# Larger and alternating chunks in four buffers, with graded ends, in a streaming softmax with relative position bias

## The chip, the cores and the metric

The kernel runs on one core of one Trainium2 chip. The metric is the device time of one execution in microseconds (us). Times are medians of several executions, with the range. An execution counts as *fast* unless it lies more than 1.5% above the fastest of the same kernel, and ratios use fast runs alone. The granted TensorE clock was 1.00 of full speed (this kernel uses no TensorE). All outputs are right.

Hardware facts below come from the profiles and traces. Where the Trainium skill (the notes on the chip) is drawn on, it is named with its page.

## The reference

The kernel adds a bias that depends only on the distance between query and key, clipped to 16, and takes a softmax over each row. All is float32.

```python
B, H, S = (2, 8, 2112); max_rel = 16
pos = np.arange(S)
rel = np.clip(pos[:, None] - pos[None, :], -max_rel, max_rel) + max_rel
logits = logits + rel_bias[:, rel][None]      # (2, 8, 2112, 2112)
logits = logits - logits.max(axis=-1, keepdims=True)
exp = np.exp(logits)
out = exp / exp.sum(axis=-1, keepdims=True)
```

There are 2 x 8 x 2112 rows of 2112 numbers (8,448 bytes). 285 MB go in and 285 MB go out, and little is computed on each number, so this is a streaming kernel. (The kernel leaves out the maximum, which these inputs don't need.)

## The kernel before

Two heads share the 128 partitions. A partition holds 33 neighbouring rows of one head; they are worked on in *chunks* of 3 rows, so a load or a store moves 128 pieces of 3 x 8,448 = 25,344 bytes. There are seven chunk buffers (`bufs=7`), hence 21 rows in memory. A buffer goes through: load, add of the bias (VectorE), three exponentials with row sums (ScalarE), reciprocal and three scalings (VectorE), store. Then the buffer is free for the load of the chunk seven later.

```python
R = 3
io = ctx.enter_context(tc.tile_pool(name="io", bufs=7))
...
NPRE = 2
pre = [load(c, nc.sync) for c in chunks[:NPRE]]       # first loads: SyncE's queue
rbB = const.tile([P, H // 2, 2, W], FP32, tag="rbB")
nc.scalar.dma_start(out=rbB, in_=...)                 # bias table
...                                                   # cut: bias_rows(k), the bias row F
for n, c in enumerate(chunks):
    k, row, j, r = c
    if k != fk:
        F, fk = bias_rows(k), k                       # every 22 chunks
    L = pre[n] if n < NPRE else load(c, nc.gpsimd)    # other loads: GpSimd's queue
    ...                                               # cut: the views L3, F3
    nc.vector.tensor_tensor(out=L3, in0=L3, in1=F3, op=ALU.add)
    tot = small.tile([P, R], FP32, tag="tot", name="tot")
    for i in range(r):
        x = L[:, i * S : (i + 1) * S]
        nc.scalar.activation(out=x, in_=x, func=EXP, accum_out=tot[:, i : i + 1])
    nc.vector.reciprocal(out=tot[:, 0:r], in_=tot[:, 0:r])
    for i in range(r):
        x = L[:, i * S : (i + 1) * S]
        nc.vector.tensor_scalar_mul(out=x, in0=x, scalar1=tot[:, i : i + 1])
    nc.sync.dma_start(out=rows(out, row, j, r), in_=L[:, 0 : r * S])   # store
```

One thing isn't visible in this text. The framework's scheduler decides in which order the instructions stand on each engine; the program text gives dependences only. An engine works through its own list in order. On VectorE the list has, for nearly all chunks, the scaling of one chunk *behind* the adds of the next two chunks.

The softmax here doesn't subtract the row's maximum and nothing guards it: scores larger than these inputs give would overflow.

Of the kernel before, what the change touches and what calls it, by code (L numbers as in the profile page):

```python
# [1 line left out]

# [4 lines left out]

FP32 = mybir.dt.float32
EXP = mybir.ActivationFunctionType.Exp
ALU = mybir.AluOpType  # L10


@with_exitstack
def kernel(
    ctx: ExitStack,
    tc: tile.TileContext,
    logits: bass.AP,
    rel_bias: bass.AP,
    out: bass.AP,
):  # L20




    nc = tc.nc
    P = 128
    B, H, S, S2 = logits.shape
    assert S == S2
    MR = 16
    W = 2 * MR + 1  # L30
    NB = S // W
    assert NB * W == S and 2 * NB == P and H % 2 == 0
    R = 3
    FW = S + W - 1

    const = ctx.enter_context(tc.tile_pool(name="const", bufs=1))
    fpool = ctx.enter_context(tc.tile_pool(name="fpool", bufs=2))
    io = ctx.enter_context(tc.tile_pool(name="io", bufs=7))
    small = ctx.enter_context(tc.tile_pool(name="small", bufs=8))

    chunks = []
    for k in range(H // 2):
        for b in range(B):
            last = k == H // 2 - 1 and b == B - 1
            sizes = [R] * (W // R)
            if last:
                sizes = sizes[:-1] + [1] * R
            j = 0
            for r in sizes:
                chunks.append((k, (b * H + 2 * k) * S, j, r))  # L50
                j += r
            assert j == W

    def rows(t, row, j, r):
        return bass.AP(
            tensor=t.tensor,
            offset=t.offset + (row + j) * S,
            ap=[[W * S, P], [1, r * S]],
        )

    def load(c, eng):
        k, row, j, r = c
        L = io.tile([P, R * S], FP32, tag="L", name="L")
        eng.dma_start(out=L[:, 0 : r * S], in_=rows(logits, row, j, r))  # L64
        return L

    NPRE = 2
    pre = [load(c, nc.sync) for c in chunks[:NPRE]]

    rbB = const.tile([P, H // 2, 2, W], FP32, tag="rbB")  # L70
    nc.scalar.dma_start(
        out=rbB,
        in_=bass.AP(tensor=rel_bias.tensor, offset=rel_bias.offset, ap=[[0, P], [1, H * W]]),
    )

    qm = const.tile([P, NB], FP32, tag="qm")
    for p0 in (0, NB):
        nc.gpsimd.iota(  # L78
            qm[p0 : p0 + NB],
            pattern=[[-1, NB]],  # L80
            base=0,
            channel_multiplier=1,
            allow_small_or_imprecise_dtypes=True,
        )
    eq = const.tile([P, NB], FP32, tag="eq")
    lt = const.tile([P, NB], FP32, tag="lt")
    gt = const.tile([P, NB], FP32, tag="gt")
    for m, op in ((eq, ALU.is_equal), (lt, ALU.is_gt), (gt, ALU.is_lt)):
        nc.vector.tensor_scalar(out=m, in0=qm, scalar1=0.0, scalar2=None, op0=op)  # L89
    rbP = const.tile([P, H // 2, W], FP32, tag="rbP")  # L90
    nc.vector.tensor_copy(out=rbP[0:NB], in_=rbB[0:NB, :, 0, :])  # L91
    nc.vector.tensor_copy(out=rbP[NB:P], in_=rbB[NB:P, :, 1, :])  # L92

    def bias_rows(k):

        F = fpool.tile([P, FW], FP32, tag="F", name="F")
        low = rbP[:, k, W - 1 : W]
        high = rbP[:, k, 0:1]
        rest = small.tile([P, NB], FP32, tag="rest", name="rest", bufs=2)
        nc.vector.tensor_scalar(out=rest, in0=lt, scalar1=low, scalar2=None, op0=ALU.mult)  # L100
        nc.vector.scalar_tensor_tensor(  # L101
            out=rest, in0=gt, scalar=high, in1=rest, op0=ALU.mult, op1=ALU.add
        )
        pitch = list(F.ap[0])[0]
        blocks = bass.AP(
            tensor=F.tensor, offset=F.offset + MR, ap=[[pitch, P], [W, NB], [1, W]]
        )
        rpitch = list(rbP.ap[0])[0]
        rev = bass.AP(
            tensor=rbP.tensor,  # L110
            offset=rbP.offset + k * W + W - 1,
            ap=[[rpitch, P], [0, NB], [-1, W]],
        )

        def wide(t):
            return bass.AP(
                tensor=t.tensor, offset=t.offset, ap=[[list(t.ap[0])[0], P], [1, NB], [0, W]]
            )

        nc.vector.tensor_tensor(out=blocks, in0=wide(eq), in1=rev, op=ALU.mult)  # L120
        nc.vector.tensor_tensor(out=blocks, in0=blocks, in1=wide(rest), op=ALU.add)  # L121
        nc.vector.tensor_copy(out=F[:, 0:MR], in_=low.to_broadcast([P, MR]))  # L122
        nc.vector.tensor_copy(out=F[:, FW - MR : FW], in_=high.to_broadcast([P, MR]))  # L123
        return F

    F, fk = None, None
    for n, c in enumerate(chunks):
        k, row, j, r = c
        if k != fk:
            F, fk = bias_rows(k), k  # L130
        L = pre[n] if n < NPRE else load(c, nc.gpsimd)
        pitch = list(L.ap[0])[0]
        L3 = bass.AP(tensor=L.tensor, offset=L.offset, ap=[[pitch, P], [S, r], [1, S]])

        F3 = bass.AP(
            tensor=F.tensor,
            offset=F.offset + W - 1 - j,
            ap=[[list(F.ap[0])[0], P], [-1, r], [1, S]],
        )
        nc.vector.tensor_tensor(out=L3, in0=L3, in1=F3, op=ALU.add)  # L140
        tot = small.tile([P, R], FP32, tag="tot", name="tot")
        for i in range(r):
            x = L[:, i * S : (i + 1) * S]
            nc.scalar.activation(out=x, in_=x, func=EXP, accum_out=tot[:, i : i + 1])  # L144
        nc.vector.reciprocal(out=tot[:, 0:r], in_=tot[:, 0:r])  # L145
        for i in range(r):
            x = L[:, i * S : (i + 1) * S]
            nc.vector.tensor_scalar_mul(out=x, in0=x, scalar1=tot[:, i : i + 1])  # L148
        nc.sync.dma_start(out=rows(out, row, j, r), in_=L[:, 0 : r * S])


# [1 line left out]
_INS = ['logits', 'rel_bias']  # L153
_OUTS = [((2, 8, 2112, 2112), 'float32')]


# [23 lines left out]
```

## Time and profile before

| | before |
|---|---|
| time | 1334.06 us (1333.89 to 1334.34, 6 runs) |
| span of the profiled run | 1332.3 us |
| VectorE busy, ScalarE busy | 71%, 39% |
| bytes moved, mean rate | 571.19 MB, 429 GB/s |
| first store issued | 57.0 us |

These are lines of the profile page of the kernel before. The row "GB/s" has 40 equal slices of the span. Below "## 5" a group reads: line, engine, operation, shapes, count, then busy time and mean nanoseconds of one, then idle time ahead of it and what ended it. Below "## 6" are transfers: count, size, median time from issue to landing.

```profile
DVE 947.2 (71%) x473; ACT 524.9 (39%) x529; POOL 49.0 (4%) x94
...
DMA  9999999999999999999999999999999999999998
GB/s 392 415 402 432 432 435 431 434 431 434 431 434 430 434 431 433 432 432 434 432 434 430 434 432 433 432 434 431 433 434 432 432 432 434 431 432 432 433 428 372
...
DMA 79%; DVE 11%; issue 7%; another core or an unknown queue 1%; ACT 0%; POOLq 0%; POOL 0%; ACTq 0%
...
L140 DVE TENSOR_TENSOR L<-L,F 128x6336 f32<-128x6336 f32 (+1 forms) x90 | 594.7, 6609 | 346.8 <-DMA L<-in_logits_dram 346.6
L148 DVE TENSOR_SCALAR L<-L,tot 128x2112 f32<-128x2112 f32 x264 | 331.8, 1313 | 0.0
...
out_dram<-L SPq DMA_DIRECT2D x87, 3168.0 KB, 38.2
L<-in_logits_dram POOLq DMA_DIRECT2D x85, 3168.0 KB, 25.7
```

The DMA engines are the limit: their row is at nine tenths throughout, the rate is flat between 430 and 435 GB/s from the fourth slice to the 38th, and the chain of waits is 79% DMA. VectorE waits for loads (346.6 us ahead of the adds).

### The profile page before, as it was taken

What the parts mean: (1) busy time and instruction counts of PE and PEld (TensorE: products, weight loads), DVE (VectorE), ACT (ScalarE), POOL (GpSimd) and SP (SyncE); (2) the same over time, 40 slices, a digit from 0 to 9 for tenths busy, and PEclk for the clock granted to TensorE, in tenths of its full rate; (3) what the DMA queues carried; (4) which work ended last, traced back from release to release, by engine and by line L of the source; (5) the groups of instructions that cost most, each with busy time, mean ns of one, the idle gap of its engine ahead of it and who ended that gap; (6) DMA issues with size and microseconds to landing.
All of it is one profiled execution on the core that took longest, in us unless ns stands there. A gap on an engine that the chain in (4) does not pass through costs nothing.

```text
span 1332.3 us, 1666 instructions
## 1 busy us (share of the span) xinstructions
DVE 947.2 (71%) x473; ACT 524.9 (39%) x529; POOL 49.0 (4%) x94
## 2 busy tenths in 40 slices
DVE  4997677669676677767966677766796677766773
ACT  0754334433344333443344333443334333443341
POOL 0000000000000000000000000000000000000000
DMA  9999999999999999999999999999999999999998
GB/s 392 415 402 432 432 435 431 434 431 434 431 434 430 434 431 433 432 432 434 432 434 430 434 432 433 432 434 431 433 434 432 432 432 434 431 432 432 433 428 372
DMA packets 26076, 571.19 MB, mean 429 GB/s; under 512 B 2896, under 2 KB 3024, under 8 KB 3024
## 3 DMA queue, kind: packets, MB, share of 16 engines
q1 hardware_dynamic: 13248, 291.97, 51.0%
q0 software_dynamic: 12672, 278.99, 48.8%
q10 hardware_dynamic: 144, 0.14, 0.0%
q14 instruction: 12, 0.10, 0.0%
HBM read 285.61 MB, written 285.47 MB: 429 GB/s over the span
## 4 chain that ended last, share of the span: by engine, by line
DMA 79%; DVE 11%; issue 7%; another core or an unknown queue 1%; ACT 0%; POOLq 0%; POOL 0%; ACTq 0%
DMA out_dram<-L 47%; DMA L<-in_logits_dram 30%; DVE L L148 6%; DVE L L140 4%; DMA rbB<-in_rel_bias_dram 1%; DVE F L121 0%; DVE F L120 0%; ACT L L144 0%; DVE tot L145 0%; POOLq L64 0%; POOL L L64 0%; DVE rest L100 0%; DVE rest L101 0%; DVE rbP L92 0%
## 5 line engine op out<-in xcount | busy, mean ns | idle before, releaser
L140 DVE TENSOR_TENSOR L<-L,F 128x6336 f32<-128x6336 f32 (+1 forms) x90 | 594.7, 6609 | 346.8 <-DMA L<-in_logits_dram 346.6
L144 ACT ACTIVATE L<-L 128x2112 f32<-128x2112 f32 x264 | 515.2, 1952 | 768.7 <-DVE L L140 756.5
L148 DVE TENSOR_SCALAR L<-L,tot 128x2112 f32<-128x2112 f32 x264 | 331.8, 1313 | 0.0
L64 POOL DMA_DIRECT2D L<-in_logits_dram x88 | 48.5, 551 | 1241.2 <-DMA out_dram<-L 1231.6
L144 ACT ACTIVATION_READ_ACCUMULATOR L<-L 128x1 f32 x264 | 49.2, 186 | 0.0
L145 DVE RECIPROCAL tot<-tot 128x3 f32<-128x3 f32 (+1 forms) x90 | 14.8, 167 | 0.9 <-ACT L L144 0.9
L91 DVE COPY rbP<-rbB 64x132 f32<-64x132 f32 x1 | 0.2, 223 | 17.9 <-DMA rbB<-in_rel_bias_dram 17.9
L121 DVE TENSOR_TENSOR F<-F,rest 128x2112 f32<-128x2112 f32 x4 | 9.4, 2344 | 0.0
L120 DVE TENSOR_TENSOR F<-eq,rbP 128x2112 f32<-128x2112 f32 x4 | 9.4, 2344 | 0.0
L144 ACT ACT_TABLE_LOAD x1 | 1.3, 1283 | 17.8 <-DMA L<-in_logits_dram 17.8
L101 DVE SCALAR_TENSOR_TENSOR rest<-gt,rbP,rest 128x64 f32<-128x64 f32 x4 | 1.0, 265 | 0.0
L100 DVE TENSOR_SCALAR rest<-lt,rbP 128x64 f32<-128x64 f32 x4 | 0.9, 240 | 0.0
L122 DVE COPY F<-rbP 128x16 f32<-128x16 f32 x4 | 0.7, 163 | 0.0
L123 DVE COPY F<-rbP 128x16 f32<-128x16 f32 x4 | 0.7, 167 | 0.0
L78 POOL IOTA qm<- 64x64 f32 x2 | 0.4, 176 | 0.4 <-PEq L175 0.4
L92 DVE COPY rbP<-rbB 64x132 f32<-64x132 f32 x1 | 0.2, 225 | 0.0
L89 DVE TENSOR_SCALAR lt<-qm 128x64 f32<-128x64 f32 x1 | 0.2, 186 | 0.0
L89 DVE TENSOR_SCALAR gt<-qm 128x64 f32<-128x64 f32 x1 | 0.2, 186 | 0.0
L89 DVE TENSOR_SCALAR eq<-qm 128x64 f32<-128x64 f32 x1 | 0.2, 185 | 0.0
L164 POOL MEMSET const-float32-0.0<- 128x1 f32 x1 | 0.1, 98 | 0.2 <-issue 0.2
L164 POOL MEMSET const-bfloat16-1.0<- 128x1 bf16 x1 | 0.1, 101 | 0.0
L164 POOL MEMSET const-float32-1.0<- 128x1 f32 x1 | 0.1, 98 | 0.0
(1 smaller groups left out, 0.1 us busy)
## 6 DMA issues: line engine op xcount, KB each, us to landing
out_dram<-L SPq DMA_DIRECT2D x87, 3168.0 KB, 38.2
L<-in_logits_dram POOLq DMA_DIRECT2D x85, 3168.0 KB, 25.7
L<-in_logits_dram SPq DMA_DIRECT2D x2, 3168.0 KB, 24.3
L<-in_logits_dram POOLq DMA_DIRECT2D x3, 1056.0 KB, 17.0
out_dram<-L SPq DMA_DIRECT2D x3, 1056.0 KB, 18.3
rbB<-in_rel_bias_dram ACTq DMA_DIRECT2D x1, 132.0 KB, 17.2
```

The source lines that it names most:

```text
L64: eng.dma_start(out=L[:, 0 : r * S], in_=rows(logits, row, j, r))
L89: nc.vector.tensor_scalar(out=m, in0=qm, scalar1=0.0, scalar2=None, op0=op)
L100: nc.vector.tensor_scalar(out=rest, in0=lt, scalar1=low, scalar2=None, op0=ALU.mult)
L101: nc.vector.scalar_tensor_tensor(out=rest, in0=gt, scalar=high, in1=rest, op0=ALU.mult, op1=ALU.add)
L120: nc.vector.tensor_tensor(out=blocks, in0=wide(eq), in1=rev, op=ALU.mult)
L121: nc.vector.tensor_tensor(out=blocks, in0=blocks, in1=wide(rest), op=ALU.add)
L122: nc.vector.tensor_copy(out=F[:, 0:MR], in_=low.to_broadcast([P, MR]))
L123: nc.vector.tensor_copy(out=F[:, FW - MR : FW], in_=high.to_broadcast([P, MR]))
L140: nc.vector.tensor_tensor(out=L3, in0=L3, in1=F3, op=ALU.add)
L144: nc.scalar.activation(out=x, in_=x, func=EXP, accum_out=tot[:, i : i + 1])
L145: nc.vector.reciprocal(out=tot[:, 0:r], in_=tot[:, 0:r])
L148: nc.vector.tensor_scalar_mul(out=x, in0=x, scalar1=tot[:, i : i + 1])
```

## The change

Its intent is to make packets larger (fewer fixed costs) and the two ends shorter:

- chunks of 5 and 6 rows alternate, in two buffers of each size (22 rows in all, much the same memory), and are still worked on in passes of up to 3 rows;
- the first chunks have 1, 2, 4, 6 ... rows, the last ones 4, 3, 2, 1, 1;
- four loads instead of two are started up front on SyncE's queue, and the bias table stands first in the program;
- the bias row has one buffer instead of two, to make room.

```diff
+    SLOT = (5, 6)
-    fpool = ctx.enter_context(tc.tile_pool(name="fpool", bufs=2))
-    io = ctx.enter_context(tc.tile_pool(name="io", bufs=7))
+    fpool = ctx.enter_context(tc.tile_pool(name="fpool", bufs=1))
+    io = ctx.enter_context(tc.tile_pool(name="io", bufs=2))
...
-            sizes = [R] * (W // R)
-            if last:
-                sizes = sizes[:-1] + [1] * R
+            sizes = [5, 6] * 3
+            if not chunks:
+                sizes = [1, 2, 4, 6, 4, 6, 4, 6]
+            if k == H // 2 - 1 and b == B - 1:
+                sizes = [5, 6, 5, 6, 4, 3, 2, 1, 1]
...
-        L = io.tile([P, R * S], FP32, tag="L", name="L")
+        size = SLOT[n % 2]
+        L = io.tile([P, size * S], FP32, tag=f"L{size}", name="L")
...
-    NPRE = 2
+    NPRE = 4          # and the table's transfer now stands ahead of these loads
...
+        for s0 in range(0, r, R):
+            w = min(R, r - s0)
             ...       # add, exponentials, reciprocal, scalings as before, on rows s0 to s0+w
         nc.sync.dma_start(out=rows(out, row, j, r), in_=L[:, 0 : r * S])
```

## The prediction

> **What bounds the kernel now.** The page's 40 slices show the 16 DMA engines at 90% or more throughout; VectorE is 71% busy, ScalarE 39%. In the stage table, 140 to 1260 us runs at DMA share 1.00 and 431 to 435 GB/s. 571.19 MB move in either kernel, so only a higher plateau or fewer idle stretches at the ends can shorten it.
>
> **Plateau.** A load or store of 3 rows gives each engine 8 packets of 25,344 B and a tiny one for the semaphore. In the trace's DMA records a packet of 25,344 B takes 0.940 us, one of 8,448 B 0.319 us: 27.21 B/ns and 8.5 ns on top of each. 16 engines at 27.21 B/ns are 435.3 GB/s, as in the Trainium skill ("DMA: Bandwidth & Descriptors", "Where 436 GB/s comes from": 16 ports x 256 bits x 850 MHz = 435.2 GB/s); the trace agrees, the load-only window 20 to 40 us shows 436. The plateau's 432.5 is 0.65% below, about 6 ns per packet (they overlap a little). With 5.5 rows to a packet the loss falls to 0.35%: 433.8 GB/s. Over 1,320 us this saves about 4 us, all on the critical path: the chain of waits is 77% loads and stores.
>
> **Ends.** At 432.5 GB/s the bytes take 1,320.7 us; the span is 1,332.3. The missing 11.6 us, by windows of 1 us: about 3 in the first 20 us; 1.3 at 56 us (all seven loads landed, first store issued at 57.0); 2.5 from 58 to 77 us (stores alone at 406 GB/s, then a dip as loads restart); 4.5 at the end (three engines finish 3 us after the others, then receipt and exit).
> The bias table lands at 17.9 us, as its small packets take turns with 25 KB packets of two queues. Its place in the program changes little: another engine issues it at the same moment (0.73 and 0.74 us). The 1-row first chunk and the absence of five early loads on the third queue matter more. Estimates: table at 5 us, bias rows done at 12, first store issued at 18 to 24 us. The four early loads (13 rows) keep the queue busy to 34 us, the stores follow without a gap, loads restart at 39 us. I expect 1 to 3 us back. The tail stays within 1 us.
>
> **What it costs.** VectorE's row work is unchanged: 6.76 us per 3 rows of add, 1.31 us per scaling, 3.6 us per row against 5.0 us of DMA. More passes and one bias buffer instead of two add some 5 us per bias rebuild, hidden under the DMA. A chunk's last scaling waits behind the next chunk's first add, hence for the next load. Estimate: 38 us from landing to store, in a cycle of 4 chunks x 27.5 us = 110 us; 72 us are left for a load and a store that need 14 us each alone, so the queues should not run dry.
>
> **Predicted time** 1,327 us; 1,322 to 1,333 should hold it 8 times in 10. Faster by over 2%: 1%; within 2%: 97%; slower by over 2%: 2%.
>
> **What would show it.** Right: packets of 42,240 and 50,688 B at 1.56 and 1.87 us; plateau 433.5 to 434.2 GB/s; table landed before 8 us; first store before 25 us; no gap before 60 us. Wrong: packets cut smaller (plateau still 432.5), or plateau slices below 430 at DMA share under 0.99 (a queue starves).
>
> **What would make it wrong.** Stretches of stores alone at 406 GB/s in every cycle (10 us slower); a new gap near 35 to 60 us as VectorE feeds the stores; a scheduling order on VectorE that holds stores back.

A note for reading it: the view by windows counts a packet whole in the window in which it begins, so its GB/s in short windows is off, in those of 1 or 2 us by several per cent. With each packet's bytes spread over its time, the loads alone (20 to 40 us) ran at 433 GB/s, which the view has as 436, and the stores alone (58 to 71 us) at 427, which it has as 406.

## More of the kernel before

A load of 3.2 MB takes 25.7 us to land and a store 38.2 us, though the 435 GB/s of all engines would move that in 7.5 us. Loads and stores flow at once and share the engines, and a transfer waits in its queue behind others of its kind.

The timeline of the kernel before, in the middle of the run (start us, length us, engine, line, operation; in brackets the idle time ahead and what ended it):

```profile
600.32 6.76 DVE L140 TENSOR_TENSOR L<-L,F 128x6336 f32<-128x6336 f32 x1 [4.45 <-DMA L<-in_logits_dram]
...
607.00 3.77 DVE L148 TENSOR_SCALAR L<-L,tot 128x2112 f32<-128x2112 f32 x3
...
610.79 38.19 SPq L149 DMA_DIRECT2D out_dram<-L  x5
...
615.33 6.76 DVE L140 TENSOR_TENSOR L<-L,F 128x6336 f32<-128x6336 f32 x1 [4.48 <-DMA L<-in_logits_dram]
...
622.01 3.77 DVE L148 TENSOR_SCALAR L<-L,tot 128x2112 f32<-128x2112 f32 x3
```

(The row of 610.79 us merges five stores; 38.19 us is the time from the first issue to the last.) VectorE waits for a load, adds, and at once scales the rows of an *older* chunk, whose exponentials had long been done; then that chunk is stored (610.79). One chunk passes every 15.0 us. A chunk is *held*, from landing to the issue of its store, for 40.5 us in this steady state. Nothing is lost by that, because seven buffers leave enough transfers in the queues.

## The result, and the profile after

| | before | after |
|---|---|---|
| time, median (range) | 1334.06 us (1333.89 to 1334.34, 6 runs) | 1354.18 us (1344.18 to 1368.56, 6 runs) |
| ratio of fast runs | | 1.0128, 95% interval 1.0095 to 1.0161 |
| first store issued | 57.0 us | 22.0 us |

A ratio is the mean time of one kernel's fast runs over the mean of the other's of the same rounds, so it is not quite the ratio of the medians quoted. Two of the six runs, 1367.14 and 1368.56 us, are left out of it as slow; they show the same clock of 1.00 as the others, and with them the ratio of the means would be 1.017. The kernel is slower by 1.3%, still "within 2%", but far outside the predicted 1322 to 1333 us. The runs of before lie within 0.5 us, those of after spread over 24 us. Again, unedited:

> The changed kernel itself, unedited, for a second trace and more times beside the variants. Theory ORDER (VectorE's program order holds finished chunks back: their last scaling stands behind both adds of the next chunk, which wait for that chunk's load) and theory COARSE (four large buffers leave too few transfers in flight, whatever the order) both expect 1344 to 1368 us as before, with the DMA loss of the first trace again after each of the three bias rebuilds (2.5 to 4 us each at about 370, 700 and 1050 us) and from 1280 us on.

Measured: 1355.85 us (1354.68 to 1356.53, four runs), ratio 1.0163 (1.0150 to 1.0176). The loss is real and repeats; its size varies. The experiments below with the labels e2 to e4 were run in the same rounds as this one (label e1).

The lines of the page of the kernel after that answer to those shown of before:

```profile
DVE 949.6 (70%) x493; ACT 524.6 (39%) x529; POOL 36.0 (3%) x55
...
DMA  9999999999999999999999999999999999999988
GB/s 396 412 443 423 438 430 434 431 432 429 434 391 431 428 431 432 436 428 429 432 428 380 430 428 429 430 437 433 428 433 422 407 442 429 437 419 436 427 351 352
...
DMA 69%; DVE 19%; another core or an unknown queue 10%; issue 1%; ACT 1%; POOL 0%; POOLq 0%; ACTq 0%
...
L148 DVE TENSOR_TENSOR L<-L,F 128x6336 f32<-128x6336 f32 (+1 forms) x100 | 594.2, 5958 | 375.8 <-DMA L<-in_logits_dram 370.0
L156 DVE TENSOR_SCALAR L<-L,tot 128x2112 f32<-128x2112 f32 x264 | 332.6, 1316 | 1.5
...
out_dram<-L SPq DMA_DIRECT2D x23, 6336.0 KB, 33.8
L<-in_logits_dram POOLq DMA_DIRECT2D x22, 6336.0 KB, 34.3
L<-in_logits_dram POOLq DMA_DIRECT2D x20, 5280.0 KB, 33.8
out_dram<-L SPq DMA_DIRECT2D x20, 5280.0 KB, 49.1
```

Work on VectorE and ScalarE is unchanged. What changed is the rate: single slices fall to 391, 380 and 407 GB/s, and two at the end to about 351. The chain is now 19% VectorE instead of 11%. And stores of 5 rows take 49.1 us to land while those of 6 rows take 33.8: the smaller ones take longer, which is a sign of queueing, not of size.

**Where the time went.** From the trace's DMA records one can work out the *lost time* of a stretch: its length less the bytes moved in it over 435.3 GB/s. 435.3 is 16 engines at the 27.21 B/ns that a packet's time shows, less its fixed 8.5 ns. For the profiled runs:

| lost us | 0 to 120 us | 120 to 1260 us | 1260 us to the end |
|---|---|---|---|
| before | 8.0 | 7.2 | 5.0 |
| after | 5.7 | 19.6 | 12.9 |
| difference | -2.3 | +12.4 | +7.9 |

The sum, +18.0 us, is the difference of the spans (1350.3 less 1332.3). The head gained as predicted. The middle and the tail lost.

**What a loss in the middle looks like.** The timeline of the kernel after around one of the dips:

```profile
325.56 50.93 SPq L157 DMA_DIRECT2D out_dram<-L  x2
...
349.10 0.53 POOL L68 DMA_DIRECT2D L<-in_logits_dram  x1 [25.90 <-DMA out_dram<-L]
356.44 6.76 DVE L148 TENSOR_TENSOR L<-L,F 128x6336 f32<-128x6336 f32 x1 [17.40 <-DMA L<-in_logits_dram]
363.12 0.22 DVE L153 RECIPROCAL tot<-tot 128x3 f32<-128x3 f32 x2
363.25 6.74 DVE L148 TENSOR_TENSOR L<-L,F 128x6336 f32<-128x6336 f32 x1
...
369.91 6.23 DVE L156 TENSOR_SCALAR L<-L,tot 128x2112 f32<-128x2112 f32 x5
...
377.42 0.53 POOL L68 DMA_DIRECT2D L<-in_logits_dram  x1 [27.80 <-DMA out_dram<-L]
```

And the DMA share (the column ahead of GB/s, the last) in three stretches of the same kernel:

```profile
365.00:370.00 5.00, 5.00 (x2) 4.23 (x6) 0.00 (x0) 1.00 1.00 433
370.00:375.00 5.00, 5.00 (x5) 4.92 (x5) 0.00 (x0) 1.00 0.77 331
375.00:380.00 5.00, 1.29 (x4) 1.03 (x2) 0.53 (x1) 1.00 0.71 297
```

Read it so. A 5-row chunk had landed at 327.7 us. Its exponentials were done by 345 us, but its last scaling stands on VectorE's list behind *both* adds of the next chunk. That chunk landed at 356.44 us, so VectorE stood idle for 17.40 us, some 12 of them with that scaling ready to be done, and scaled only from 369.91 us. The first line counts two stores issued from 325.56 to 376.5 us: the earlier at 325.6, the next only at 376.2. The store queue ran dry from about 370 us. By itself that cost nothing: the one load in flight now had the engines to itself, and they still moved 434 GB/s until 374 us. But this load ended the sooner for it, and the next could be issued only at 377.42 us, when the store of 325.6 us had landed (376.8 us) and its buffer was free. So both queues were thin at once, and from 374 to 378 us only 225 GB/s moved. (These rates spread each packet's bytes over its time; the view, which counts a packet where it begins, has shares of 0.77 and 0.71.)

This is the same order on VectorE as in before (older chunk's scaling behind newer adds). So the order alone can't be the reason; the question is why it hurts now.

**The budget of a buffer.** For the chunks loaded from 120 to 1180 us the traces give these means (range in brackets). "Load" is issue to landing, "hold" is landing to issue of the store, "waits" is the store's issue to its first packet, that is the time in the queue, "moves" is its first packet to its last.

| us | load | hold | store waits | store moves | sum |
|---|---|---|---|---|---|
| before, 7 buffers | 25.8 | 39.2 (18.4 to 41.5) | 22.5 (19.8 to 43.7) | 15.4 | 103.0 |
| after, 4 buffers | 33.8 | 36.6 (21.6 to 49.6) | 10.2 (0.8 to 25.3) | 28.1 | 108.7 |

The column "store waits" is the slack. In before a store always finds more than a whole transfer ahead of it (19.8 us at least). In after a larger transfer moves for 28.1 us because loads and stores flow at once, so only 10 us of slack are left. The hold varies by 28 us, its longest is 13 us above its mean, and in some cycles the store waits 0.8 us: it finds the queue empty. In before the hold varies too, by 23 us, but mostly downwards: its longest is only 2.2 us above the mean. (A load's wait in its queue, part of "load", is 8.8 us in before and 5.1 us in after.)

### The profile page after: what moved, and what is told of

Same layout as the page of the kernel before. It is cut to its first block, busy times and chain, and to the rows that moved or that the text cites. A ratio compares the mean times of both kernels' runs of the same rounds, so it can differ in the third digit from the quotient of the medians.

```text
span 1350.3 us, 1475 instructions
## 1 busy us (share of the span) xinstructions
DVE 949.6 (70%) x493; ACT 524.6 (39%) x529; POOL 36.0 (3%) x55
## 4 chain that ended last, share of the span: by engine, by line
DMA 69%; DVE 19%; another core or an unknown queue 10%; issue 1%; ACT 1%; POOL 0%; POOLq 0%; ACTq 0%
DMA L<-in_logits_dram 37%; DMA out_dram<-L 31%; DVE L L148 12%; DVE L L156 6%; ACT L L152 1%; DMA rbB<-in_rel_bias_dram 0%; DVE F L125 0%; DVE F L124 0%; POOL L L68 0%; DVE tot L153 0%; POOLq L68 0%; DVE rest L104 0%; DVE rest L105 0%; DVE rbP L96 0%
## 5 line engine op out<-in xcount | busy, mean ns | idle before, releaser
L68 POOL DMA_DIRECT2D L<-in_logits_dram x49 | 35.5, 724 | 1288.6 <-DMA out_dram<-L 1135.1
## 6 DMA issues: line engine op xcount, KB each, us to landing
out_dram<-L SPq DMA_DIRECT2D x23, 6336.0 KB, 33.8
L<-in_logits_dram POOLq DMA_DIRECT2D x20, 5280.0 KB, 33.8
out_dram<-L SPq DMA_DIRECT2D x20, 5280.0 KB, 49.1
```

The costliest lines, as they stand in the source:

```text
L68: eng.dma_start(out=L[:, 0 : r * S], in_=rows(logits, row, j, r))
```

## The experiments

Two more measures from the trace's DMA records are used, both between about 90 and 1260 us. A *dry spell* is a time in which one of the two queues (loads or stores) has, averaged over 2.5 us, less than one packet in flight on all 16 engines together. (The count depends on how the average is taken; a recount for after gave 53 instead of 46.) *Stretch* is the time that packets take beyond their normal time, added up and divided by 16 engines. Before has 1 dry spell and 0.3 us of stretch, after 46 dry spells (115 us in all) and 10.4 us. Of that stretch 8.5 us lie from 2 us ahead of the start to 10 us behind the end of a dry spell, a region that covers 46% of the time. A dry spell doesn't itself idle the engines, as just seen: it tells that one queue alone is left to feed them. Nor is it shown that dry spells cause the stretch: in scale first, below, only some 0.1 of 4 us of stretch lies near them.

The theories: the order on VectorE holds finished chunks too long and unevenly; or there are too few buffers left over; or it is the single bias buffer, the graded tail, or the length of the transfers. The texts give them short names: ORDER, HOLD (long holds) and UNEVEN (uneven holds) are about the order; COARSE and COUNT are about too few buffers; TAIL is about the graded tail; PACKET and LENGTH are about long transfers, and EARLY is the rival of LENGTH, that half of a chunk leaves earlier. A label such as e2 in these texts is that of a run; it stands beside the run's heading here.

### The order on VectorE

**Scale first (e2).** Before the next chunk's adds may stand on VectorE's list, this chunk's last scaling must. (`issue_after` puts an instruction behind another one in its engine's list.)

```diff
+            with tc.issue_after(done.ins) if done is not None else nullcontext():
                 nc.vector.tensor_tensor(out=L3, in0=L3, in1=F3, op=ALU.add)
...
+        done = last_ins          # the chunk's last scaling
         nc.sync.dma_start(out=rows(out, row, j, r), in_=L[:, 0 : r * S])
```

> One edit: each chunk's adds are placed after the last scaling of the chunk before, in VectorE's program order. Buffers, chunk sizes and transfers stay. ORDER: the stalls after the three rebuilds vanish (about 10 us) and part of the tail's (up to 6 us): 1336 to 1342 us, spread of the runs below 5 us. COARSE: 1350 to 1358 us with the same stalls and the same spread. A third possibility: VectorE now waits for ScalarE inside each chunk and becomes the limit, over 1360 us.

Measured: 1341.81 us (1337.91 to 1342.71), ratio 1.0052 (1.0039 to 1.0065). The hold fell to 21.7 us (19.5 to 25.7), a store now waits 11.9 us and never less than 3.4, and 6 dry spells were left of 46. The lost time in the middle went from 19.6 us (26.4 in the second trace of after) to 7.9 us, nearly that of before (7.2). The time and its spread are what ORDER expected, except that it expected a gain at the tail too. The GB/s row of its page has no dips in the middle, only at the end:

```profile
GB/s 399 415 432 438 431 429 431 439 433 429 437 437 429 434 436 430 431 431 431 440 431 430 430 436 429 421 437 437 425 429 437 433 431 431 436 430 430 430 394 281
```

So with these buffers and transfers the order is the cause of the loss in the middle. The tail is not mended (14.4 us lost).

**Scale late (e7).** The opposite: every chunk's last scaling is put behind both adds of the next chunk.

```diff
+        if pend is not None:                 # the previous chunk
+            with tc.issue_after(add.ins):    # this chunk's last add
+                scale(*pend[:4])
+            store(*pend[4:])
```

> The reverse of e2: the changed kernel with the last scaling of every chunk placed after both adds of the next one, so that all are held alike (about 48 us from landing to store, where the changed kernel has 22 to 49 in turn). If the length of the hold itself starves the queues (theory HOLD), the loss is now in every cycle: 1370 us or more. If it is the uneven spacing of the stores (theory UNEVEN: in the changed kernel 50 us pass between two issues of stores after a rebuild), the plateau is clean as in e2 and only head and tail cost: 1340 to 1352 us.

Measured: 1386.01 us (1375.21 to 1388.76), ratio 1.0377. The hold is 46.0 us, a store waits 5.3 us (0.8 to 13.8), 38.7 us are lost in the middle, 31 of them as stretch. HOLD expected 1370 us or more, UNEVEN 1340 to 1352 us. The row of its page:

```profile
GB/s 390 423 434 400 439 433 432 411 420 415 425 427 430 426 423 435 417 427 436 376 409 434 398 393 435 429 418 415 435 389 439 429 404 398 430 424 432 343 366 394
```

Hold up by 9 us, slack down by 5, time up by 32 us: holds that are long in every cycle are enough for a loss, and it fits that the slack is what matters. (With short transfers the same order costs far less; see "Long or short transfers".)

**Scale first, in the kernel before (e8).**

> The kernel before (3 rows, seven buffers) with the same edit as e2. There the scaling stands behind two adds of later chunks too, yet the engines run at a share of 1.00. All theories expect no change in the plateau: 1331 to 1336 us. If the kernel before gained 5 us or more, the order would have been costing time there as well and the account of its 11.6 us of losses (head and tail only) would be wrong.

Measured: 1505.65 us (1504.81 to 1505.79), ratio 1.1286. No theory had this right; it is a miss, and a useful one. The timeline of VectorE in this run:

```profile
593.70 6.75 DVE L142 TENSOR_TENSOR L<-L,F 128x6336 f32<-128x6336 f32 x1
606.52 0.18 DVE L147 RECIPROCAL tot<-tot 128x3 f32<-128x3 f32 x1 [6.06 <-ACT L L146]
606.73 3.78 DVE L150 TENSOR_SCALAR L<-L,tot 128x2112 f32<-128x2112 f32 x3
610.42 6.75 DVE L142 TENSOR_TENSOR L<-L,F 128x6336 f32<-128x6336 f32 x1
```

With 3-row chunks there is nothing else to do while ScalarE works, so the add (6.75), ScalarE (6.06) and the scaling (3.78) stand one behind the other: 16.7 us per chunk against 15.0 us of transfer, and the chain of engines becomes the limit. The scheduler's order, scaling behind later adds, is right for 3-row chunks. In a chunk of 5 or 6 rows the two passes overlap each other, and the same edit helped.

### The number of buffers

**Five buffers instead of seven in the kernel before (e10).** If slack is what is missing, the kernel before must show the same symptom when slack is taken from it, with its small packets and its regular order.

```diff
-    io = ctx.enter_context(tc.tile_pool(name="io", bufs=7))
+    io = ctx.enter_context(tc.tile_pool(name="io", bufs=5))
```

> The kernel before with five buffers of 3 rows instead of seven; packets stay 25,344 B. About 2.3 chunks are held for work there, so 2.7 buffers are left for loads and stores, near the 2.2 of the changed kernel (4 less 1.8). COUNT: one queue runs dry again and again, packets are stretched when it restarts, the time rises by 10 us or more and spreads by several us, with small packets. PACKET: within 5 us of the kernel before and as steady.

Measured: 1376.19 us (1368.83 to 1377.74), ratio 1.0298 (1.0274 to 1.0322). A store waits 8.1 us (1.9 to 15.0) in place of 22.5. There are 29 dry spells and 17.2 us of stretch, 17.0 of it within the same distance of dry spells as above (36% of the time). The lost time in the middle is 27.5 us, and 21.8 us in the head, where five loads end long before the first store. The GB/s row shows both:

```profile
GB/s 394 236 405 436 428 436 422 436 430 419 424 434 400 431 433 418 430 434 431 407 435 425 416 433 430 404 422 433 432 398 432 433 403 433 431 434 407 427 434 352
```

So neither large packets nor uneven chunks are needed for a loss, as COUNT expected and PACKET did not; too little slack is enough. Even the larger spread between runs (9 us instead of 0.5) comes with it.

### The bias buffer

**Two bias buffers in the kernel after (e3).** The dips at 360, 700 and 1050 us come right after the bias row is rebuilt, and there the order differs (a 5-row chunk behind both adds of the next).

```diff
-    fpool = ctx.enter_context(tc.tile_pool(name="fpool", bufs=1))
+    fpool = ctx.enter_context(tc.tile_pool(name="fpool", bufs=2))
```

> One edit: two bias buffers again instead of one (it fits). In the built program this alone removes the places after a rebuild where a chunk of 5 rows is scaled behind both adds of the next chunk of 6. ORDER: the stalls after the rebuilds vanish, the tail stays: 1341 to 1348 us. COARSE: no change, 1350 to 1358 us.

Measured: 1360.09 us (1352.74 to 1377.45; the slowest of the six counts as slow), ratio 1.0188, not told apart from after in the same rounds (1.0163). A miss for the theory that the single buffer costs time. The losses after rebuilds did shrink (in the windows 320 to 420, 640 to 760 and 980 to 1080 us: 1.6, 3.0 and 1.6 us instead of 4.2, 5.3 and 2.9), but others appeared elsewhere: 6-row chunks were now held behind both adds of the next chunk, and stores came in pairs, with 6.6 and 56 us between them. The rebuild is where one bad order sat, not the cause.

### The tail

**Even chunks to the end (e4)**, and the same with scale first (e5).

```diff
-            if k == H // 2 - 1 and b == B - 1:
-                sizes = [5, 6, 5, 6, 4, 3, 2, 1, 1]
```

> One edit: the last batch is cut into 5 and 6 rows to its end like the others, no 4, 3, 2, 1, 1. If the graded tail is what costs the 8 us after 1260 us (its loads wait for the store four chunks back, and each is small), this gains up to 5 us: about 1349 us. If it helps as intended, the 6-row chunk at the end costs its scaling and 15 us of store: 1356 to 1365 us. The stalls after the rebuilds stay in either case.

> e2 (scalings first) with the last batch cut into 5 and 6 rows to its end. In e2 the DMA engines lost 14 us after 1260 us, against 5 in the kernel before: each of its last loads (3, 2, 1, 1 rows) is issued only when the store four chunks back has landed. Theory TAIL (the small chunks sit in the same four buffers, so they do not bring more work into the queues, only less): the tail's loss falls to 6 to 9 us, 1333 to 1337 us in all. Rival (grading is right, the loss comes from elsewhere): the 6-row chunk at the end adds 10 us or more, 1350 us.

Measured: 1351.03 us (1344.91 to 1358.66) and 1342.76 us (1334.07 to 1343.92), ratios 1.0128 and 1.0052: neither can be told from its partner (after, 1.0128 and in the same rounds 1.0163; scale first, 1.0052). In the first the tail's lost time fell to 7.3 us, but its profiled run was the slowest of six (32 us lost in the middle), so the parts can't be weighed against each other. In the second the tail still lost 14.3 us; an explanation is that the last 6-row store starts only when all six rows are scaled. It was expected at 1333 to 1337 us: a miss.

**Scale first, even chunks, and the last chunk stored in three pieces (e6).**

```diff
+        split = n == len(chunks) - 1
+        for s0, w in ((0, 3), (3, 2), (5, 1)) if split else ...:
             ...
+            if split:
+                nc.sync.dma_start(out=rows(out, row, j + s0, w), in_=L[:, s0 * S : (s0 + w) * S])
```

> e5 with the very last chunk of 6 rows stored in three pieces (3, 2, 1 rows) as they are scaled; it is still loaded whole. TAIL: the engines stay busy to the end, the loss after 1260 us is 4 to 6 us as in the kernel before; 1329 to 1333 us, 1 to 4 us below the kernel before. Rival: no better than e5.

Measured: 1336.23 us (1331.44 to 1341.38), ratio 1.0022 (1.0003 to 1.0041). The tail lost 9.9 us, 4.4 less than with even chunks alone, which bears the explanation out in part; both the time and the tail stay above what was expected (1329 to 1333 us, 4 to 6 us). So the store in pieces helps at the end, and grading the chunks gained nothing over even ones (14.4 against 14.3 us lost). In scale first the last loads, of 3, 2, 1 and 1 rows, were issued only at 1258.9, 1280.6, 1301.7 and 1315.5 us, each when the store four chunks earlier had landed. A small chunk takes a whole buffer, so with four buffers the DMA engines have little to do while small chunks pass. No run tests this reading by itself.

### Long or short transfers

**Pieces of at most 3 rows (e9).** The same as the last, with each chunk's load and store split into transfers of at most 3 rows.

```diff
-        eng.dma_start(out=L[:, 0 : r * S], in_=rows(logits, row, j, r))
+        for s0 in range(0, r, R):
+            w = min(R, r - s0)
+            eng.dma_start(out=L[:, s0 * S : (s0 + w) * S], in_=rows(logits, row, j + s0, w))
...       # cut: the stores likewise
```

> e6 (scalings first, even last batch, last chunk stored in pieces) with every load and store issued as pieces of at most 3 rows; buffers and order stay, only packets are 25,344 B or less again and a pass can start on its own piece. Theory PACKET (packets of 42 to 51 KB are themselves what is stretched and what lets the 16 engines drift apart): the stretched packets (2 to 6 us of mean engine time between 100 and 1260 us in e5 and e6) vanish, all runs lie within 2 us, 1331 to 1334 us. Theory COUNT (what matters is how many buffers are left over for the two queues): the same spread and mean as e6 within 3 us, perhaps 2 us slower by the packets' fixed cost.

Measured: 1333.37 us (1332.85 to 1335.84), ratio 0.9997 (0.9983 to 1.0010). One dry spell, 0.24 us of stretch; level with before. The stretch is gone, as PACKET expected; the time fits both theories (COUNT allowed 3 us around the run before it).

**The late order with such pieces (e12).**

> e7 (every last scaling after both adds of the next chunk) with every load and store issued as pieces of at most 3 rows, as e9 is to e6; VectorE's order is the same as in e7 from the first bias batch's end to the last batch. It asks how much of e7's 52 us over the kernel before is the long packets' doing. PACKET: nearly all of it, 1335 to 1345 us, stretched packets below 3 us of mean engine time between 100 and 1260 us (31 in e7). COUNT and HOLD (a queue runs dry because too few of the four buffers are left over): still 1360 us or more, with the queues dry at the same rate and packets stretched at each restart.

Measured: 1339.23 us (1337.01 to 1344.20), ratio 1.0034, against 1.0377 with whole chunks. But here a pass can start when its own piece has landed, so the late order itself is milder. Four further runs lay the order on VectorE down instruction by instruction, once late (e13, e14) and once as in the kernel after (e15, e16), each with whole transfers and with pieces (upper rows worked on first, so that the first add waits for both loads).

> A control for e14: every last scaling behind both adds of the next chunk, as in e7, VectorE's order laid down fully; loads and stores of whole chunks (packets of up to 50,688 B). Both theories: like e7, 1365 to 1395 us, with dry queues and over 20 us of stretched packets between 100 and 1260 us.

> e13 with each load and store cut into two pieces, packets of at most 25,344 B, and nothing else: VectorE's program order is the same in the built programs, and of each chunk the piece that lands last is worked on first, so the first add still waits for the whole chunk and both stores still follow the last scaling. PACKET (the long packets let the engines drift apart, stretch, and so drain the queues): 1335 to 1348 us, stretch below 5 us. HOLD (time from landing to store with only four buffers): within 10 us of e13, 1360 us or more; then e12 was fast because its passes started before the whole chunk had landed.

> A control for e16: the changed kernel with, for every chunk, the number of adds of the next chunk (0, 1 or 2) that its last scaling stands behind laid down as the scheduler had chosen it; whole chunks. Both: near the changed kernel, 1345 to 1360 us.

> e15 with each load and store cut into two pieces as in e14, the first add still waiting for the whole chunk. This asks of the changed kernel itself what its long packets cost at its own holds. PACKET: 1334 to 1341 us, half or less of the loss above the kernel before. HOLD: within 5 us of e15.

| ratio (interval) | whole transfers | pieces |
|---|---|---|
| late order | 1.0258 (1.0214 to 1.0302) | 1.0031 (1.0019 to 1.0043) |
| order of after | 1.0239 (1.0211 to 1.0267) | 1.0179 (1.0162 to 1.0197) |

Two of the six runs of the late order with whole transfers counted as slow (1389.53 and 1383.52 us). The two controls did not come out like the runs that they copy: 1.0258 against 1.0377 in scale late, and 1.0239 against 1.0128 and 1.0163 in after (1364.76 us, above the 1345 to 1360 us expected). Why is not known, so the table is to be read along its rows. In the late order pieces took back nearly all the loss, as PACKET expected; in the order of after they came out between the two theories. The trace then showed that one line of what had been expected was false: the first of the two stores had *not* stayed behind the chunk's last scaling. The scheduler had moved it ahead (in the lower right run a store was issued at 463.3 us whose chunk was scaled at 481.7 us). So two things had changed at once: transfers were shorter, and half of each chunk left earlier. Two last runs (e17, e18) take that apart. One column is copied onto itself after the last scaling, which makes the first store wait for it, and the second store is the one for which the next load waits first; so each wait is as with whole transfers, and only the cut is left.

```diff
+        if r > R:
+            with tc.issue_after(scaled):
+                nc.vector.tensor_copy(out=L[:, 0:1], in_=L[:, 0:1])
+        low = None
+        for s0, w in pieces(r):
+            with tc.issue_after(low) if low is not None else nullcontext():
+                low = nc.sync.dma_start(
+                    out=rows(out, row, j + s0, w), in_=L[:, s0 * S : (s0 + w) * S]
+                ).ins
```

> e13_late_long with each chunk's load and store cut into two transfers of at most 3 rows and nothing else: the order of VectorE is that of e13, both stores are issued only after the chunk's last scaling (a copy of one column after it makes the first store wait), the second store reaches the rows whose next load is issued first, so both loads wait for both stores; the chunk's first add waits for the load issued last. In e14_late_short the first store had slipped ahead of the last scaling, so two causes were mixed. LENGTH (short packets are what helps): 1335 to 1348 us as e14 (1338), packets stretched by under 4 us in all, fewer than 20 episodes in which one queue has no packet. EARLY (what helped in e14 was that half of a chunk was stored early): 1360 to 1390 us as e13 (1375), packets stretched by 15 to 30 us, 40 or more episodes. Both: in between.

> e15_order_long (VectorE's order of the changed kernel laid down) cut in the same way, both stores after the last scaling, both loads after both stores. LENGTH: at or below e16_order_short, 1345 to 1360 us, packets stretched by under 12 us. EARLY: at or above e15, 1360 to 1378 us, stretched by 20 us or more. If e17 says LENGTH and this stays near 1360, the uneven order costs some 20 us of idle queues whatever the packets are.

Measured: late order 1342.83 us (1340.15 to 1344.72), ratio 1.0066 (1.0049 to 1.0083); order of after 1363.27 us (1359.21 to 1364.98), ratio 1.0210 (1.0191 to 1.0229). The GB/s rows of the late order, first with whole transfers, then cut:

```profile
GB/s 391 432 425 436 426 440 415 409 424 415 433 432 426 424 441 420 422 403 436 410 422 423 407 392 437 417 409 438 428 429 400 409 416 430 408 426 434 406 421 295
```

```profile
GB/s 388 418 429 426 434 431 431 432 433 426 432 431 431 427 429 434 433 430 429 431 430 431 430 432 429 433 430 432 430 429 434 428 435 430 426 435 430 411 422 360
```

In the late order the cut by itself is worth about 2 points of the ratio: the lost time in the middle fell from 36.2 to 12.2 us and the stretch from 28.5 to 4.5 us, which is what the theory LENGTH expected (stretch a little above its bound of 4, and 56 dry spells where it expected fewer than 20, though they are shorter: 68 us in all instead of 113). In the order of after the cut brought nothing that can be told from the spread (1.0210 against 1.0239, the intervals overlap; 133 and 135 us in dry spells), and the run is above the range that LENGTH gave and inside EARLY's. Its stretch, 13.5 us, lies between the two expectations. The early half store (and the swapped order of the rows) goes with another 0.3 points in both orders (1.0066 to 1.0031, and 1.0210 to 1.0179; the intervals of the second pair just overlap).

What follows: the late order comes at regular intervals (16 to 39 us between stores), and there short transfers help. The order of after is irregular (6.6 to 60.4 us in the earlier run with pieces), and there a queue runs dry for long, whatever the size of the transfers. Why a dry spell is shorter and milder with short transfers stays open: the kernel before with five buffers has short packets too and yet 192 us of dry spells and 17 us of stretch.

### The head by itself

**The graded head in the kernel before (e11)**, with seven loads up front and nothing else of the change.

```diff
+            if not chunks:
+                sizes = [1, 2] + [R] * (W // R - 1)
...
-    NPRE = 2
+    NPRE = 7
```

> The kernel before with only a graded head: first chunks of 1 and 2 rows, and the first seven loads all on the SP queue so that two queues, not three, are active at the start. Expected of the part of the change that helps: bias table at 7 us instead of 17.9, first store issued before 35 us instead of 57, the loss before 120 us falls from 8.0 to about 5.5 us, the plateau and the tail stay: 1330.5 to 1332.5 us, spread below 1 us. If the head's gain is eaten by later stalls: 1334 us.

Measured: 1331.21 us (1331.12 to 1331.83, five runs), ratio 0.9978 (0.9965 to 0.9990). Lost time in the head 4.7 us instead of 8.0, the rest unchanged (7.2 and 5.1). Its row of GB/s, to be held against the first slices of before (392 415 402):

```profile
GB/s 389 432 430 434 429 435 432 434 432 432 433 430 436 430 436 429 434 430 435 431 435 431 432 434 431 435 431 432 432 433 433 432 433 431 435 432 435 431 429 369
```

This version beats both kernels, before by 0.2% and after by 1.5% (1.0128 over 0.9978). It is the one part of the change that was worth keeping; the small first chunks and the single queue of first loads weren't tried apart.

## Why the prediction was wrong, point by point

- **Total.** Predicted 1327 us (1322 to 1333), measured 1354.18. The class "within 2%" was right only because the loss happened to be small; the sign was wrong.
- **Packets: right.** Packets of 42,240 and 50,688 B took 1.561 and 1.872 us (predicted 1.56 and 1.87).
- **Plateau gain of 4 us: it was there, but given back.** Scale first, with its long packets and few dry spells, lost 7.9 us from 120 to 1260 us. Of these 4.2 are stretch; the other 3.7 are close to the 0.35% predicted (4.0 us of 1140). Before lost 7.2 us there, nearly all fixed costs. So larger packets saved some 3 us (7.2 less 0.3 of stretch, against 3.7) and slow packets took 4.2.
- **Ends: the head right, the tail wrong.** The table landed at 7.4 us (predicted below 8), the first store was issued at 22.0 us (18 to 24), and 2.3 us came back (1 to 3). "The tail stays within 1 us" failed: it lost 7.9 us more. The prediction gave no reason for that line and didn't ask what it means that small chunks occupy whole buffers.
- **The step that failed**, as the prediction put it: "72 us are left for a load and a store that need 14 us each alone, so the queues should not run dry." The hold (estimate 38 us, measured mean 36.6) and the cycle (110 us, measured 108.7 in the four parts) were right. The mis-sized term is 14 us each *alone*: in the middle of the run loads and stores flow together. Measured, a load took 33.8 us to land and a store moved for 28.1 us, twice the 14. With the hold that makes 98.5 of 108.7 us, so 10 us of slack where the prediction counted 44 (72 less 28). The page of before had the warning: a 3-row load, 7.5 us alone, took 25.7 us.
- **A second omission** is that the hold was taken as one number. It ran from 21.6 to 49.6 us, and the longest holds, 13 us above the mean, don't fit into 10 us of slack. The list of what would make the prediction wrong did name "a scheduling order on VectorE that holds stores back", and that is what happened, but nothing had been worked out for it, and a range that ended at 1333 us left it no room.
- **The signs of "wrong" appeared**: slices at 391, 380 and 407 GB/s, and a share of 0.71 to 0.77 in the window shown.
- **What is shown and what isn't.** Shown: with four buffers and long transfers the order on VectorE causes the loss in the middle (scale first removes it, scale late raises it), little slack is enough for a loss (five buffers), the bias buffer isn't the cause, the head's gain is separate. Shown too: long transfers have a part in it, for in the late order the cut alone took the loss in the middle from 36.2 to 12.2 us. Not settled: what in the DMA engines or the memory stretches packets, near a dry spell or elsewhere, why short transfers ease the late order and not the other, and how the loss of the tail divides between small chunks and last stores.

The Trainium skill, "DMA: Bandwidth & Descriptors", section "Queues, rings and completion order", says that an engine goes round the queues that have work, packet by packet. The trace agrees: a store of before moves its 3.2 MB in 15.4 us, twice the 7.5 us that it would need alone. The prediction used that to explain the late table, and not for the budget. The same page's section "Bandwidth" advises transfers of at least 1 MiB; the chunks of both kernels are well above (3.2 against 5.4 to 6.5 MB), and the step from the one to the other brought no net gain. The page "Trainium Kernel Development and Optimization", section "Best Practices", says to double-buffer so that DMA overlaps with compute; the kernel after has two buffers of each size, and they were not enough with these holds (46 dry spells).

## What to carry to other kernels

Before trading many small buffers for a few large ones, add up a buffer's cycle: load and store at the rate that they get while both directions flow (read it from the transfers' time to landing in the profile, not from bytes over peak rate), plus the hold from landing to store. What is left of the cycle is the queue's slack. In the profiled runs worked out here it had to exceed what the longest hold has above the mean, not only be positive: in before 2.2 us stood against 22.5 of slack and in scale first 4.1 against 11.9, without loss; in after 13.0 against 10.2, in scale late 9.8 against 5.3, and with five buffers 9.1 against 8.1, each with loss. That is a pattern in five runs, not a rule that was tested; with short transfers no such sum was made. Read the engine's real instruction order before blaming or praising it: the same order was needed with 3-row chunks and did harm with 5 and 6. And undo a compound change part by part: its head alone was a gain.

## What the Trainium skill lacked or had wrong

- "DMA: Bandwidth & Descriptors", section "Where 436 GB/s comes from": its 435.2 GB/s agrees (27.21 B/ns on each of 16 engines, 435.3). The page's figure of about 10.5 ns for a packet (section "Bandwidth") is from a transfer of 4 KB; it has none measured on large packets, and here the fixed part was 8.5 ns on a packet of 25,344 B that takes 0.940 us.
- The same page, "Queues, rings and completion order": nothing on what happens when one of two queues runs dry. Here packets near such moments took up to 1.7 us longer (17.0 of 17.2 us of stretch in the run with five buffers lay near dry spells).
- The same page, "Bandwidth": the rule of at least 1 MiB per transfer has no upper side. Here 5.4 to 6.5 MB in four buffers gave 1.0128 of the time of 3.2 MB in seven (size and count of buffers changed together).
- "Trainium Kernel Development and Optimization", "Best Practices": double-buffering has no rule for how many buffers. Here seven buffers gave 1 dry spell, and five gave 29 and 2.98% more time.
- No page that was read tells that the order in which a scheduler lists instructions on VectorE can decide the DMA rate: scale first and scale late differ by 44 us (1341.81 and 1386.01) with the same work.
